# A second layer's modulation vectors, moved from the context's stages to the first layer's latent attention, in half-width blocks

## The chip, the cores and the metric

The kernel runs on one core of a Trainium2 chip. A core has five engines that work side by side, each with an instruction queue of its own: TensorE (PE, matrix products; its weight loads are listed apart as PEld), VectorE (DVE), ScalarE (ACT), GpSimd (POOL) and SyncE (SP), which here issues nearly all loads and stores. The metric is the time of one execution in microseconds (us) on the device.

## What is computed

Two layers of a diffusion backbone over 512 latent tokens and 256 context tokens of 1024 channels. Cut to what matters:

```python
for l in range(2):
    mod_lat = silu(c) @ w_ada[l] + b_ada[l]            # six vectors of 1024 for the latent tokens
    mod_ctx = silu(c_ctx) @ w_ada[l] + b_ada[l]        # and six for the context
    sh1, sc1, g1, sh2, sc2, g2 = split(mod_lat)
    xn = rms(x, norm1_g[l]) * (1 + sc1) + sh1          # modulated norm; the same for the context
    y_lat, y_ctx = token_mix(xn, hn, ...)              # attention, pooling, recurrence (mLSTM)
    x = x + g1 * (y_lat @ w_out[l])
    x = x + g2 * peer(rms(x, norm2_g[l]) * (1 + sc2) + sh2, ...)   # 16384 experts, product-key routing
    # in the first layer the context goes the same way
```

The change concerns `silu(c) @ w_ada[l] + b_ada[l]` of the second layer (l = 1): a matrix of 1024 x 6144 numbers in float32 (24 MB), applied to two vectors.

## The kernel before

`main` (L1498) traces the program. Work is written as Python generators, each `yield` a step, and these are advanced beside each other; a planner then orders the instructions on every engine at build time by their priority in the program and by what it takes to be ready. So the order on an engine isn't exactly the program's.

The generator `ada` (L268) computes the modulation vectors of one layer. A part is one of the six vectors; a block is half a part, 512 columns. For each block it loads 1024 x 512 weights (`wa`, 2 MB, three buffers, two loads ahead), multiplies them with the two conditioning vectors on PE (eight blocks of rows, four of them side by side in a quarter of the array each), copies the sums to `row` on ACT or DVE, and sums the four quarters with small products on PE. Shifts and scales (parts 0, 1, 3, 4) become columns in `modT`, by an addition on DVE; gates (parts 2 and 5) become rows `gr`, with a bias row `bb` that is loaded, and are stored to DRAM (`grow`). The sums take one of four banks `mm` and one of two banks `tr` of PSUM, which all other work in this stage uses too. Every product goes through `mm` (L142), every load and store by SP through `load` (L200), every copy through `copy` (L130, L132).

In the first layer `main` does this (L1508 to L1540):

1. Context: its norm, then `ada` parts 0 and 1 of layer 0, then its projections. `self.bg` holds a chain of the rest of layer 0's `ada` (8 blocks) and all of layer 1's (12 blocks). Each step of the projections advances it by 0.7 steps, each step of the core (the context's attention `na_core` and recurrence `mlstm` in turn) by 0.5; `run(ada)` finishes it.
2. `project_ctx`: the context's output projection. From here to the end of the context's routing (`peer_ctx`) the latent generator `lat` (projections, gates, then `na_core` of the latent tokens, 20 steps) advances in the background, by the amount of foreground products.
3. A loop over what is left of `lat`, the latent attention; each step advances the recurrence `rest` of the latent tokens by 0.4 steps.
4. `project`: the output projection of the latent tokens, with the remaining recurrence inside it; then `peer_lat`, the experts, which takes most of the layer.

A step of `na_core` has three kinds of PE work: `scores` (products of `qT` with `kT` and with the context's `kTc`), `turn` (transposes of the softmax `prob` into `probT`) and `values` (products of `probT` with V). Its softmax runs on DVE, ACT and POOL. For each new head pair `head` loads two `bias` tiles.

SBUF tiles come from pools on two stacks, left and right. A pool opened later lies above, and takes over the place of pools closed before it once their last users are done. In stage 1 the pools of `ada` are on the right. The recurrence of step 3 and `px` (the latent stream `xt`) are on the left.

Of the kernel before, what the change touches and what calls it, by code (L numbers as in the profile page):

```python
# [19 lines left out]
DRAM = bass.MemoryType.DRAM  # L20

P = 128
D = 1024
# [18 lines left out]
# latent tokens whose experts are computed densely, per layer; the rest gathers expert rows  # L42
# [22 lines left out]
# candidate pairs (a, b) of two sorted lists with (a + 1)(b + 1) <= 16: (first a, number of a, number of b, offset)  # L65
# [10 lines left out]
def merge(*gens):  # L76
    """Steps of several generators in turn."""
    gens = list(gens)
    while gens:
        for g in list(gens):  # L80
            try:
                yield next(g)
            except StopIteration:
                gens.remove(g)


class Kern:
# [57 lines left out]
    def tick(self, us):  # L145
        """Advance the background work by what fits beside `us` of foreground work."""
        if self.rate and self.bg:
            self.clock += us * self.rate
            while self.clock >= 1.0 and self.bg:
                self.clock -= 1.0  # L150
                self.step()
# [18 lines left out]
    def steps(self, n):  # L170
        """Advance the background work by n steps."""
# [5 lines left out]
    def flush(self):  # L177
        """Finish the gathers under way without starting others."""
# [5 lines left out]
    def advance(self, n):  # L184
        """Advance the second background work by n steps."""
# [29 lines left out]
    # ------------------------------------------------------------------ setup  # L215
# [34 lines left out]
    def xsrc(self, l, w, seg, i, cols=slice(0, D)):  # L250
        """Residual stream before sub-layer w of layer l: 128 tokens of a segment."""
# [15 lines left out]
    # -------------------------------------------------------------------- ada  # L267
    def ada(self, l, parts, pw, ps):  # L268
        """Modulation vectors: shifts and scales as columns, gates as rows in DRAM."""
        nc, a = self.nc, self.a  # L270
        slot = {0: 0, 1: 1, 3: 2, 4: 3}

        def fetch(j):
            w = self.T(pw, [P, KD, 512], tag="wa", bufs=ADA_BUFS)
            self.load(w, a["w_ada"][l, :, j * 512:(j + 1) * 512].rearrange("(k p) n -> p k n", p=P))
            return w

        order = [2 * part + half for part in parts for half in range(2)]
        ahead = [fetch(order.pop(0)) for _ in range(ADA_BUFS - 1)]
        for part in parts:  # L280
            for half in range(2):
                j = 2 * part + half
# [3 lines left out]
                # a quarter of the array for each of four blocks of the contraction  # L286
                acc = self.ps("mm")
# [3 lines left out]
                row = self.T(ps, [P, 512], tag="row")  # L291
                self.copy(row, acc)
                pt = self.ps("tr")
                if part in slot:
                    for q in range(4):
                        self.mm(pt[:, q * 2:q * 2 + 2], row[:, q * P:(q + 1) * P], self.sel)
                    nc.vector.tensor_add(
                        self.modT[l][:, slot[part], half * 4:half * 4 + 4, :],
                        pt[:, :8].rearrange("p (k v) -> p k v", v=2),
                        self.bcols[:, l, part, half * 4:half * 4 + 4, None].to_broadcast([P, 4, 2]))  # L300
                else:
                    bb = self.T(ps, [2, 512], tag="bb")
                    self.load(bb, a["b_ada"][l:l + 1, j * 512:(j + 1) * 512].to_broadcast([2, 512]))
                    self.mm(pt[:2], self.sel, row)
                    gr = self.T(ps, [2, 512], tag="gr")
                    nc.vector.tensor_add(gr, pt[:2], bb)
                    self.load(self.grow[l][part // 5][:, half * 512:(half + 1) * 512], gr)
# [7 lines left out]
    # ------------------------------------------------------------ adaLN norms  # L315
    def parts(self, pool, src, cols, tag, eng, bufs):
        """Half a block of weights in the two parts that float32r products carry: a pair for each 128 rows."""
# [7 lines left out]
    def norm(self, l, w, seg, xT, xt=None, side=None, deep=2):  # L325
        """Modulated norm, channel-major, of the residual stream, in one part or two.

        xt: the stream [P, n / P, D] and partial sums of its squares [P, n / P, 4], where those are on chip."""
# [40 lines left out]
    # ------------------------------------------------------------- token mix  # L369
# [3 lines left out]
    def store(self, l, seg, full, st, m, alias=False):  # L373
        """What outlives the projections, in a pool for each of three stacks."""
# [25 lines left out]
    def projections(self, l, seg, full, m):  # L400
        """The projections of a segment, a generator that takes a block of weights in each step."""
# [17 lines left out]
    def latent(self, l, m):  # L419
        """The first layer's latent projections, then their attention where the projections' operand was."""  # L420
# [6 lines left out]
    def mlstm(self, l, seg, full, m):  # L427
        """The recurrence after the projections, a generator."""
# [12 lines left out]
    def project_ctx(self, l, m):  # L441
        """The context's new residual stream, to DRAM."""
# [20 lines left out]
    def project(self, l, m, px, sd, rest=()):  # L463
        """The latent tokens' new residual stream, to DRAM and to a pool, after the rest of their mixing."""
# [41 lines left out]
    def weights(self, l, full, pool):  # L506
        """Blocks of columns of w_in (256, the gates 100), each a step; half a block ahead of its use."""
# [20 lines left out]
    def mm3(self, out, lhs, rhs):  # L528
        """Contraction over blocks of operands that are given in two parts each."""
# [1139 lines left out]
```

## Time and profile before

| | |
|---|---|
| median of 3 runs | 4576.12 us (4574.12 to 4580.28) |
| span of the profiled execution | 4588.3 us |
| PE busy | 4041.2 us (88%) |
| DVE busy | 3483.2 us (76%) |
| POOL busy | 2233.7 us (49%) |
| ACT busy | 1761.3 us (38%) |
| HBM traffic | 216 GB/s over the span |
| PE's mean granted clock | 0.932 of full speed |

The profile comes from one execution. Its page cuts the span into 40 slices of 115 us; a digit is the busy share in tenths. The granted clock of PE is a share of 2.4 GHz. A view of windows gives the busy time of each engine in a stretch; a timeline gives start, length, engine, line, operation, the tile written and the tiles read, how many instructions were merged (x), and in brackets how long the engine stood idle before and what ended that. The ends of products are modelled, so the distance of starts tells more than a length.

### The profile page before, as it was taken

To read this page: it belongs to the slowest core of one execution; us is meant where nothing else is said; L and a number is where in the kernel's file an instruction comes from. 1 tells how busy PE (TensorE), PEld (TensorE's weight loads), DVE (VectorE), ACT (ScalarE), POOL (GpSimd) and SP (SyncE) were. 2 spreads that over 40 slices of the span, in tenths; PEclk is the share of its full clock that TensorE was granted. 3 is DMA by queue.
4 is the path that set the end of the run, shared out by engine and by line. 5 is a ranking of instruction groups with operands and counts; after the bars stand their busy time and mean duration, and the time that the engine had idled before them with its cause. 6 is when DMAs were issued, how large, how long until landed. Compare 5 with 4: busy or idle time off the path is not lost. (4 is left out here: it accounts for less than half of the span.)

```text
span 4588.3 us, 57862 instructions
## 1 busy us (share of the span) xinstructions
PE 4041.2 (88%) x20829; PEld 3367.6 (73%) x20829; DVE 3483.2 (76%) x6158; ACT 1761.3 (38%) x2754; POOL 2233.7 (49%) x1552
## 2 busy tenths in 40 slices
PE   6889777877779999999999979888868899999998
PEld 4568667756657777777777768677657788888887
DVE  2545675789979999889999855674889678887776
ACT  2332243335543333333333333343246344444343
POOL 2133355776645555455555333345866344444441
PEclk8889888988889999999999989988978999999999
DMA  7663212327778888788888633223256777777784
GB/s 270 215 211 93 81 48 82 94 94 227 219 268 303 323 316 317 301 316 316 322 316 317 257 113 109 63 73 98 71 171 206 263 294 291 286 301 296 277 304 166
DMA packets 429352, 996.51 MB, mean 217 GB/s; under 512 B 31448, under 2 KB 264280, under 8 KB 375816
## 3 DMA queue, kind: packets, MB, share of 16 engines
q1 hardware_dynamic: 372760, 586.46, 37.0%
q0 software_dynamic: 56304, 406.35, 24.2%
q8 instruction: 164, 2.69, 0.2%
q14 instruction: 124, 1.02, 0.1%
HBM read 909.97 MB, written 81.17 MB: 216 GB/s over the span
## 5 line engine op out<-in xcount | busy, mean ns | idle before, releaser
L1227 POOL TENSOR_TENSOR eacc<-eacc,uv 128x1024 f32<-128x1024 f32 x189 | 587.2, 3107 | 1074.1 <-ACT uv L1226 1013.4
L1240 DVE SCALAR_TENSOR_TENSOR uv<-uv,xn 128x1024 f32<-128x1024 f32 x384 | 849.8, 2247 | 0.0
L142 PE MATMUL o<-dvh,dch 128*128 128x512 f32 x1792 | 709.0, 396 | 72.3 <-DVE do L1436 53.2
L142 PE MATMUL o<-dvh,dcl 128*128 128x512 f32 x1792 | 706.0, 394 | 0.7 <-DVE dcl L1473 0.7
L142 PE MATMUL o<-dvl,dch 128*128 128x512 f32 x1792 | 704.9, 393 | 0.0
L1258 POOL DMA_INDIRECT uv<-in_peer_uv_dram,ridx x384 | 579.7, 1510 | 137.2 <-issue 75.0
L1394 PE MATMUL h<-xh,duh 128*128 128x512 f32 (+1 forms) x1632 | 607.7, 372 | 37.2 <-ACT duh L1388 35.8
L1394 PE MATMUL h<-xh,dul 128*128 128x512 f32 (+1 forms) x1632 | 607.6, 372 | 0.4 <-DVE dul L1389 0.3
L1394 PE MATMUL h<-xl,duh 128*128 128x512 f32 (+1 forms) x1632 | 606.0, 371 | 0.0
L142 PEld LDWEIGHTS o<-dvh,dch 128*128 128x128 f32 x1792 | 337.2, 188 | 162.1 <-DVE do L1436 64.6
L142 PEld LDWEIGHTS o<-dvh,dcl 128*128 128x128 f32 x1792 | 338.2, 189 | 86.9 <-DVE dcl L1473 14.6
L142 PEld LDWEIGHTS o<-dvl,dch 128*128 128x128 f32 x1792 | 337.5, 188 | 66.7 <-DVE dvl L1462 0.3
L1394 PEld LDWEIGHTS h<-xh,duh 128*128 128x128 f32 x1632 | 312.6, 192 | 80.4 <-ACT duh L1388 36.4
L1462 DVE TENSOR_TENSOR dvl<-dv,dvh 128x1024 fp32r<-128x1024 f32 x256 | 309.8, 1216 | 62.5 <-ACT dvh L1461 62.4
L1389 DVE TENSOR_TENSOR dul<-du,duh 128x1024 fp32r<-128x1024 f32 x204 | 249.5, 1224 | 135.0 <-ACT duh L1388 128.2
L1388 ACT CAST duh<-du 128x1024 fp32r<-128x1024 f32 x256 | 267.6, 1046 | 202.7 <-PE h L1394 102.1
L1394 PEld LDWEIGHTS h<-xl,duh 128*128 128x128 f32 x1632 | 312.1, 191 | 43.6
L1394 PEld LDWEIGHTS h<-xh,dul 128*128 128x128 f32 x1632 | 311.2, 191 | 39.7 <-DVE dul L1389 1.6
L142 PE MATMUL mm<-go,gob 128*128 128x128 f16 x1792 | 239.9, 297 | 96.9 <-DVE go L1366 85.4
L1244 ACT ACTIVATE egf<-dots 128x2 f32<-128x2 f32 x192 | 39.1, 204 | 734.8 <-DVE uv L1240 734.8
L1472 ACT CAST dch<-dcf 128x512 fp32r<-128x512 f32 (+1 forms) x256 | 145.2, 567 | 437.1 <-DVE dcf L1469 434.8
L1461 ACT CAST dvh<-dv 128x1024 fp32r<-128x1024 f32 x256 | 263.2, 1048 | 112.1 <-DMA dv<-in_peer_v_dram 63.4
(356 smaller groups left out, 8785.2 us busy)
## 6 DMA issues: line engine op xcount, KB each, us to landing
du<-in_peer_ut_dram SPq DMA_DIRECT2D x256, 512.0 KB
dv<-in_peer_v_dram SPq DMA_DIRECT2D x256, 512.0 KB
Gd<-gst SPq DMA_DIRECT2D x28, 2048.0 KB
wa<-in_w_ada_dram SPq DMA_DIRECT2D x24, 2048.0 KB
w<-in_w_in_dram SPq DMA_DIRECT2D x78, 512.0 KB
dG<-Gd SPq DMA_DIRECT2D x32, 1024.0 KB
w<-in_peer_wq_dram SPq DMA_DIRECT2D x48, 512.0 KB
dG<-Gd SPq DMA_DIRECT2D x32, 768.0 KB
```

The costliest lines, as they stand in the source:

```text
L142: self.nc.tensor.matmul(out, lhsT=lhsT, rhs=rhs, start=start, stop=stop)
L1227: nc.gpsimd.tensor_add(acc[1], acc[1], V)
L1240: nc.vector.scalar_tensor_tensor(t[:, :D], t[:, :D], 1.0, xn, op0=OP.mult, op1=OP.mult, accum_out=dots[:, k:k + 1])
L1244: nc.scalar.activation(ge, x, AF.Gelu_apprx_tanh)
L1258: nc.gpsimd.indirect_dma_start(t, None, a["peer_uv"], bass.IndirectOffsetOnAxis(ap=idx[:, k:k + 1], axis=0))
L1388: nc.scalar.copy(uh, u)
L1389: eng.tensor_sub(ul, u, uh.bitcast(F32))
L1394: nc.tensor.matmul(hp[:, :nd], lhsT=lt[:, k], rhs=rt[:, k, :nd], start=n == 0, stop=n == 3 * KD - 1)
L1461: nc.scalar.copy(vh, v)
L1462: nc.vector.tensor_sub(vl, v, vh.bitcast(F32))
L1472: m1 = nc.scalar.copy(ch, cf)
```

## The change

`ada` gets the number of buffers and the width of a block as arguments (`bufs=ADA_BUFS, n=512`), and loops over columns in steps of `n`. In the context's stage only layer 0's eight remaining blocks are left in the background; the calls that advance them stay. Layer 1's six parts are computed in the loop over the latent attention, in 24 blocks of 256 columns (1 MB each) with two buffers (one load ahead), one block with each step of `lat`, and what is left right after the loop. Its two pools are opened on the left, after a first step of `rest` that opens the recurrence's pools below them. Comments are dropped from the file as well, which shifts lines.

```diff
-    def ada(self, l, parts, pw, ps):
+    def ada(self, l, parts, pw, ps, bufs=ADA_BUFS, n=512):
...
-        def fetch(j):
-            w = self.T(pw, [P, KD, 512], tag="wa", bufs=ADA_BUFS)
-            self.load(w, a["w_ada"][l, :, j * 512:(j + 1) * 512].rearrange("(k p) n -> p k n", p=P))
+        nq = n // P
+
+        def fetch(c):
+            w = self.T(pw, [P, KD, n], tag="wa", bufs=bufs)
+            self.load(w, a["w_ada"][l, :, c:c + n].rearrange("(k p) n -> p k n", p=P))
             return w
...
-        ahead = [fetch(order.pop(0)) for _ in range(ADA_BUFS - 1)]
+        order = [part * D + c for part in parts for c in range(0, D, n)]
+        ahead = [fetch(order.pop(0)) for _ in range(bufs - 1)]
         for part in parts:
-            for half in range(2):
-                j = 2 * part + half
+            for c in range(0, D, n):
                 w = ahead.pop(0)
                 if order:
                     ahead.append(fetch(order.pop(0)))
...
-                acc = self.ps("mm")
+                acc = self.ps("mm")[:, :n]
                 for k in range(KD):
                     g = 32 * (k % 4)
                     self.mm(acc[g:g + 32], self.sc[:, k, :], w[:, k, :], k < 4, k >= 4)
-                row = self.T(ps, [P, 512], tag="row")
+                row = self.T(ps, [P, n], tag="row")
                 self.copy(row, acc)
                 pt = self.ps("tr")
                 if part in slot:
-                    for q in range(4):
+                    for q in range(nq):
                         self.mm(pt[:, q * 2:q * 2 + 2], row[:, q * P:(q + 1) * P], self.sel)
...
                 else:
...
-                    self.mm(pt[:2], self.sel, row)
-                    gr = self.T(ps, [2, 512], tag="gr")
-                    nc.vector.tensor_add(gr, pt[:2], bb)
-                    self.load(self.grow[l][part // 5][:, half * 512:(half + 1) * 512], gr)
+                    self.mm(pt[:2, :n], self.sel, row)
+                    gr = self.T(ps, [2, n], tag="gr")
+                    nc.vector.tensor_add(gr, pt[:2, :n], bb)
+                    self.load(self.grow[l][part // 5][:, c:c + n], gr)
                 yield
...
-                    ada = chain(self.ada(0, (2, 3, 4, 5), pw, ps), self.ada(1, range(6), pw, ps))
+                    ada = self.ada(0, (2, 3, 4, 5), pw, ps)
                     self.bg = [ada]
...
                 rest = self.mlstm(l, 0, True, ml)
-                for _ in lat:
-                    self.some(rest, ML_CORE)
+                next(rest)
+                with ExitStack() as s2:
+                    pw, ps = self.pool(s2, "adaw", 1, side="left"), self.pool(s2, "adas", 1, side="left")
+                    ada = self.ada(1, range(6), pw, ps, 2, 256)
+                    for _ in lat:
+                        next(ada, 0)
+                        self.some(rest, ML_CORE)
+                    run(ada)
                 sl.pop().close()
```

## Rows read from the trace of the kernel before

**Rows 1.** The page: span, and busy tenths and granted clock in 40 slices

```profile
span 4588.3 us, 57862 instructions
PE   6889777877779999999999979888868899999998
PEclk8889888988889999999999989988978999999999
```

**Rows 2.** Windows: stretch, its length, busy us (x instructions) by engine, clock, DMA share, GB/s

```profile
173.00:272.00 99.00, 85.57 (x567) 51.45 (x565) 50.36 (x169) 34.53 (x86) 20.02 (x34) 0.88 0.72 245
...
200.00:264.00 64.00, 62.96 (x458) 37.81 (x462) 37.93 (x136) 24.25 (x69) 16.64 (x26) 0.97 0.77 271
```

**Rows 3.** The same windows, of instructions on tile wa, then on tile row alone

```profile
173.00:272.00 99.00, 27.73 (x192) 5.62 (x192) 0.88 0.72 245
...
173.00:272.00 99.00, 12.86 (x72) 9.15 (x72) 2.77 (x4) 4.69 (x8) 0.88 0.72 245
```

**Rows 4.** Timeline of PE in the context's core: start, us, engine, line, operation, out<-in

```profile
188.88 3.64 PE L142 MATMUL mm<-wa,sc 128*32 128x512 f32 x16
...
199.89 2.07 PE L142 MATMUL mm<-kTc,qT 128*128 128x256 f32 x4 [0.56 <-ACT qT L988]
...
215.38 1.92 PE L142 MATMUL mm<-wa,sc 128*32 128x512 f32 x16
217.23 0.49 PE L142 MATMUL sm<-va,kw 128*128 128x130 f32 x2
...
218.42 0.95 PE L142 MATMUL tr<-sel,row 128*128 128x2 f32 x8
219.30 0.66 PE L142 MATMUL sm<-probT,Vc 128*64 128x128 f32 x8
...
250.48 1.03 PE L142 MATMUL mm<-kTc,qT 128*128 128x256 f32 x4
...
254.46 1.16 PE L142 MATMUL sm<-va,ww 128*128 128x130 f32 x8
...
257.99 1.92 PE L142 MATMUL mm<-wa,sc 128*32 128x512 f32 x16
...
272.71 13.62 PE L142 MATMUL mm<-w,yT 128*128 128x256 f32 x48 [2.17 <-DMA w<-in_w_out_dram]
```

**Rows 5.** Windows of the latent attention, columns as in rows 2

```profile
626.00:640.00 14.00, 12.83 (x101) 9.72 (x100) 10.41 (x27) 8.52 (x23) 6.76 (x11) 0.96 0.74 187
640.00:690.00 50.00, 49.11 (x408) 41.06 (x407) 40.68 (x109) 27.09 (x66) 24.42 (x25) 1.00 0.12 32
690.00:740.00 50.00, 37.63 (x259) 35.54 (x260) 37.00 (x105) 13.17 (x24) 27.59 (x24) 0.86 0.25 80
600.00:626.00 26.00, 12.87 (x69) 8.77 (x68) 24.27 (x60) 6.67 (x17) 19.27 (x24) 0.69 0.23 61
```

**Rows 6.** Timelines of DVE and of SP's queue at the end of the context's core

```profile
263.04 1.13 DVE L860 SCALAR_TENSOR_TENSOR yT<-tr,mng,og 128x128 f32<-128x128 f32 x4 [0.17 <-PE tr L197]
...
264.65 0.88 SPq L200 DMA_DIRECT2D w<-in_w_out_dram  x1
267.76 3.77 SPq L200 DMA_DIRECT2D grow<-gr  x2
```

**Rows 7.** Timelines of PE and of SP's queue in the latent attention

```profile
636.53 0.66 PE L142 MATMUL sm<-probT,VW 128*64 128x128 f32 x8
637.02 0.61 PE L142 MATMUL sm<-probT,Vc 128*64 128x128 f32 x8
...
700.18 2.10 PE L142 MATMUL sm<-va,ww 128*128 128x130 f32 x8 [4.58 <-DVE dn L819]
...
622.84 2.51 SPq L200 DMA_DIRECT2D xt<-in_x_dram  x4
...
686.23 43.52 SPq L200 DMA_DIRECT2D w<-in_w_out_dram  x7
```

**Rows 8.** Timeline of POOL at the start

```profile
0.99 0.55 POOL L638 MEMSET gif<- 36x256 f32 x2
```

More of the change, by code (lines that the diff above doesn't have):

```diff
@@ L1 @@
 from contextlib import ExitStack
-from itertools import chain
 import numpy as np
@@ L265, in xdst @@
                        ap=[[D, 16], [GW * D, GR], [1, cols.stop - cols.start]])
-    def ada(self, l, parts, pw, ps):
+    def ada(self, l, parts, pw, ps, bufs=ADA_BUFS, n=512):
         nc, a = self.nc, self.a
         slot = {0: 0, 1: 1, 3: 2, 4: 3}
-        def fetch(j):
-            w = self.T(pw, [P, KD, 512], tag="wa", bufs=ADA_BUFS)
-            self.load(w, a["w_ada"][l, :, j * 512:(j + 1) * 512].rearrange("(k p) n -> p k n", p=P))
-            return w
-        order = [2 * part + half for part in parts for half in range(2)]
-        ahead = [fetch(order.pop(0)) for _ in range(ADA_BUFS - 1)]
+        nq = n // P
+        def fetch(c):
+            w = self.T(pw, [P, KD, n], tag="wa", bufs=bufs)
+            self.load(w, a["w_ada"][l, :, c:c + n].rearrange("(k p) n -> p k n", p=P))
+            return w
+        order = [part * D + c for part in parts for c in range(0, D, n)]
+        ahead = [fetch(order.pop(0)) for _ in range(bufs - 1)]
         for part in parts:
-            for half in range(2):
-                j = 2 * part + half
+            for c in range(0, D, n):
                 w = ahead.pop(0)
@@ L294, in ada @@
                 if part in slot:
-                    for q in range(4):
+                    for q in range(nq):
                         self.mm(pt[:, q * 2:q * 2 + 2], row[:, q * P:(q + 1) * P], self.sel)
+                    ks = slice(c // P, c // P + nq)
                     nc.vector.tensor_add(
-                        self.modT[l][:, slot[part], half * 4:half * 4 + 4, :],
-                        pt[:, :8].rearrange("p (k v) -> p k v", v=2),
-                        self.bcols[:, l, part, half * 4:half * 4 + 4, None].to_broadcast([P, 4, 2]))
-                else:
-                    bb = self.T(ps, [2, 512], tag="bb")
-                    self.load(bb, a["b_ada"][l:l + 1, j * 512:(j + 1) * 512].to_broadcast([2, 512]))
-                    self.mm(pt[:2], self.sel, row)
-                    gr = self.T(ps, [2, 512], tag="gr")
-                    nc.vector.tensor_add(gr, pt[:2], bb)
-                    self.load(self.grow[l][part // 5][:, half * 512:(half + 1) * 512], gr)
+                        self.modT[l][:, slot[part], ks, :],
+                        pt[:, :2 * nq].rearrange("p (k v) -> p k v", v=2),
+                        self.bcols[:, l, part, ks, None].to_broadcast([P, nq, 2]))
+                else:
+                    bb = self.T(ps, [2, n], tag="bb")
+                    self.load(bb, a["b_ada"][l:l + 1, part * D + c:part * D + c + n].to_broadcast([2, n]))
+                    self.mm(pt[:2, :n], self.sel, row)
+                    gr = self.T(ps, [2, n], tag="gr")
+                    nc.vector.tensor_add(gr, pt[:2, :n], bb)
+                    self.load(self.grow[l][part // 5][:, c:c + n], gr)
                 yield
```

## Prediction, made before the changed kernel was run

> **What bounds the kernel now.** I read the page first: the span and the slices of the TensorE (PE) and of its granted clock [rows 1]. PE is busy 88% of the span, and the first seven slices (115 us each) hold everything the change touches: the context's first sub-layer, the latent tokens' projections beside the context's routing, then the latent attention. Nothing after about 770 us is edited. So two stretches have to be priced, and the question for each is whether PE is the limit there.
>
> The first is the context's core (attention and recurrence of the context), about 200 to 264 us. The view of windows gives PE 62.96 us of 64, VectorE (DVE) 37.93, and 271 GB/s of loads [rows 2]: PE sets the pace. The 12 blocks of the second layer's modulation vectors start at 188.88 us, and the last of them ends just ahead of 272.71 [rows 4]; in 173 to 272 their products take 27.73 us of PE and the small products on `row` behind them 12.86 us, of 85.57 us busy in all [rows 2, 3]. The timeline of PE shows how they lie in the queue: a full block at 215.38 lets the next product start 1.85 us later, its transposes at 218.42 hold the queue for 0.88 us [rows 4], together 2.73 us, and the engine goes from one to the next without a gap.
>
> The second is the latent attention, where the blocks go. From 640 to 690 us PE is busy 49.11 us of 50 at clock 1.00, with DVE at 40.68; from 626 to 640 PE has 12.83 of 14 [rows 5]. So the blocks go from one stage that PE limits to another one. Idle PE lies at its two ends: 13.1 us in 600 to 626, where DVE is busy 24.27 of 26 us with the end of the context's routing, and 12.4 us in 690 to 740, where the recurrence's last steps hang on DVE [rows 5].
>
> **What is removed from the context's core.** Of the 12 blocks, nine lie between 200 and 263 us: 9 x 2.73 = 24.6 us of a queue that is full. Without them 62.96 - 24.6 = 38.4 us of PE remain, and about 33 of DVE (37.93, less 2.77 for copies of `row` [rows 3] and about as much for the additions behind them, an estimate). PE is therefore still the largest, but no longer without gaps: the attention's softmax and the recurrence's chain become visible. I go by the distance of the attention's steps: eight steps of scores start from 199.89 to 250.48 us [rows 4], 7.2 us each. One block less in each gives 7.2 - 2.73 = 4.5; in 626 to 640, a mixed stretch without any of these blocks, PE is 92% busy [rows 5], and 4.5 / 0.92 = 4.9. Eight steps (seven distances and the outputs behind the last) save 8 x 2.3 = 18 us. Bounds: nothing hidden, 24.6; a step of 6 us, 9.6. I take 18, since PE has 38 us of work against 33 of DVE and the queue has nothing else to wait for in order.
>
> The core's tail saves nothing: from the last products at 254.46 to the last of `yT` at 263.04 [rows 4, 6] a chain of short DVE operations runs, and the block at 257.99 lay beside it. The last two blocks and their gates come after it and beside the wait for the output projection's weights: those are issued at 264.65 and PE starts on them at 272.71 [rows 4, 6], 8.1 us for 1 MB. At 271 GB/s [rows 2] 1 MB takes 3.9 us; the rest is the second layer's blocks still in flight. Saved: 4 us (0 to 5). SP's queue also stood 3.77 us at the two stores of `gr` at 267.76 [rows 6], with the context's rows, the latent tokens' x and the next weights queued behind; without them the latent norm comes forward. Saved: 3 us (0 to 6). The first block at 188.88 takes 3.64 us at half clock beside the gates' chain on DVE: nothing (0 to 2). Together **-25 us**, with ends at -10 and -37. What is late next is the context's output projection, which simply starts earlier, and all behind it shifts with it.
>
> **What is added to the latent attention.** Each block becomes two of 256 columns. A half block keeps 16 product instructions (8 row blocks, two passes each) of half the columns, and has half of the transposes. Half of 2.73 is 1.37 us. The instruction count could set a floor: eight products on `probT` let the next eight start 0.49 us later (636.53 to 637.02 [rows 7]), 0.061 us each, so 16 take 0.98 us, and with 0.5 for the transposes 1.5 us. I take **1.4 us**, near the first end, as 0.93 us of columns for 16 instructions is just under that floor. 24 of them are 33.6 us (33 to 36).
>
> How many fall in the loop follows from the code. The ticks in `project_ctx` (64 products of 0.427 us at rate 0.2: 5.5) and in the routing (16 x 3.84 us at 0.25: 15.4) advance the latent generator 20 steps. It has 17 before the attention and 20 in it, so 17 steps remain in the loop, and 17 half blocks go with them; 7 are left for `run(ada)` behind the loop.
>
> Loop: 17 x 1.4 = 23.8 us, less the idle PE of 626 to 690, 1.2 + 0.9 us [rows 5]: **+22 us**. The 13.1 us idle in 600 to 626 I don't count as cover: the pool of the weights stands on the left stack above `px` and the recurrence's tiles, and `px`'s loads are issued from 622.84 us on [rows 7], when the routing's tiles there are done. The first half block would so arrive at about 628. If its place were free earlier, up to 9 half blocks could fit, -13.
>
> Behind the loop: 7 x 1.4 = 9.8 us in 12.4 us of idle PE. Half of it finds the gaps where the recurrence waits for DVE (one is 4.58 us, at 700.18 [rows 7]), some pushes that chain: **+3 us** (0 to 9.8).
>
> The rest: 24 copies of `row` on ACT and DVE, additions, and on SP 24 loads of 1 MB, 8 of `bb`, 8 stores of `gr`. DVE has 9 us spare in 640 to 690, DMA is 12% busy there [rows 5]. Waits are the danger: with two buffers a load waits on SP until the block before the last has been multiplied, and behind it are queued `bias` for the next head and, after 686.23, the output projection's weights [rows 7]. The store of `gr` waits for DVE in the same queue. PE then waits for `bias` through POOL and DVE. I take **+2 us** (0 to 8). Together **+27 us**, with ends at +12 and +44.
>
> Nothing else changes: the eight blocks of the first layer stay in the context's projections, and the second layer's vectors are needed only in the second layer, far behind.
>
> **Sum.** -25 + 27 = +2 us. The profiled execution took 4588.3 us [rows 1], 0.27% above the median of 4576.12 (4574.12 to 4580.28); the sum is a difference of stages and goes on the median: **4578 us**. A measurement of this kernel tells about 0.2% (9 us) from no change.
>
> **Rivals.** *The gaps take more than I count* (faster). The order on an engine is not the program's but a planner's, which pulls ready work forward: POOL clears the recurrence's `gif` at 0.99 us [rows 8], some 100 us before its use. If it puts four or five half blocks into 600 to 626 (-7), all seven last ones into 690 to 740 (-3), and the latent norm into the now open ends of the context's core (-6), the change is worth -14: 4562. For it: 25 us of idle PE at the right places. Against: the left stack's place seems not free before 622 us.
>
> *The clock falls in the context's core* (slower). Where PE is busy half of the time, its granted clock is lower: 12.87 of 26 us at 0.69 in 600 to 626, against 1.00 in 640 to 690 [rows 5]. The core would keep 38.4 us of work in some 46, 83%, and decides by whether its gaps are bunched. Should it get 0.75, the 38.4 us become 51: even a full queue would save only 13 us, with the chains' waits 10 (a step of 6 us), and the latent norm could no longer use the 3 us: -10 - 4 + 0 + 27 = +13, 4589. The point from which it decides is a clock below about 0.85 between 200 and 250 us. The Trainium skill, "TensorE: Matmul & The Clock Gate" (Part 1: The HAM clock gate), says that the throttled clock is the default and only sustained work lifts it, so that work taken out of a stream can make what is left slower. By that rule these blocks were also what kept the core at 0.97, and the time would be the 4589 of this rival. The rows bear it out in part: the stretch 626 to 640, 92% busy, still has 0.96.
>
> *The two buffers hold up SP's queue* (slower). If a load regularly stands in front of `bias` or the output projection's weights, three heads lose 3 us each and the weights 4: +2 + 13 = 4591. It decides when half blocks come faster than 1 MB lands (3.9 us at 271 GB/s, 8.1 at worst [rows 2, 4, 6]); steps of about 5.9 us speak against it.
>
> *It doesn't do what it says*: the planner lets most half blocks drift behind the loop. Then 33.6 us less the 12.4 idle, +21 in place of +27: 4572, no change either.
>
> **How the numbers follow.** Forecast 0.40, drift 0.04: within 0.2% together 0.44. Gaps 0.28: faster. Clock 0.20 and queue 0.08: slower 0.28. The range takes in the two outer cases with some of their spread: 4556 to 4597; the likeliest case alone spans 4568 to 4587.
>
> **What would show it.** In the profile after: no 512-wide products on `wa` behind about 173 us; score steps of the context about 4.9 us apart at a clock above 0.9; the context's output projection starting near 250 and not at 272.71; 384 products of 256 columns on `wa` between about 628 and 730; the attention's PE-full stretch some 22 us longer. Wrong: context steps of 6 us or a clock below 0.85 (rival two), half blocks before 620 (rival one), SP's `bias` landing late with PE waiting on DVE's addition (rival three). The forecast falls if either stretch is off by more than 9 us without the other following.

## The result and the profile after

The changed kernel takes 4614.89 us (median of 4 runs, 4611.04 to 4617.29), against 4576.99 us of the kernel before beside it: a ratio of 1.008 with a 95% interval from 1.0066 to 1.0095. It is 38 us slower, and lies above the forecast's range.

The page after shows little of it: against [rows 1], TensorE's busy tenths fall in the fifth slice (461 to 577 us) and rise in the sixth and the eleventh; the differences in the 25th to 27th come from all work there being later.

```profile
span 4614.4 us, 58329 instructions
...
PE   6889687877879999999999978978868899999998
...
PEclk8889888888889999999999989989878999999999
```

To find the 38 us I follow four marks through both traces: the end of the context's routing on TensorE (the last transposes of its `xT`), the last scores of the latent attention (`kT`,`qT`), the issue of `gB` (output projection of the latent tokens) and the issue of `iotac` (start of the latent tokens' routing). The first and last mark before:

```profile
598.41 0.62 PE L197 MATMUL tr<-ident,xT 128*128 128x128 f32 x4
...
773.40 0.33 SPq L200 DMA_DIRECT2D iotac<-in_iota_dram  x1
```

The two between, before, on TensorE's timeline and on SyncE's queue (the second of the pair of score products starts at 675.8):

```profile
675.56 0.59 PE L142 MATMUL mm<-kT,qT 128*128 128x256 f32 x2
...
685.86 0.33 SPq L200 DMA_DIRECT2D gB<-grow  x1
```

All four, after (start, length, engine, line, operation, tile written and read, instructions merged; brackets: idle time before, and what ended it), on TensorE's timeline:

```profile
193.04 3.16 PE L141 MATMUL mm<-kTc,qT 128*128 128x256 f32 x8
...
224.99 1.03 PE L141 MATMUL mm<-kTc,qT 128*128 128x256 f32 x4
...
246.66 22.20 PE L141 MATMUL mm<-w,yT 128*128 128x256 f32 x94 [0.50 <-DMA w<-in_w_out_dram]
...
566.16 0.63 PE L196 MATMUL tr<-ident,xT 128*128 128x128 f32 x4
566.62 0.43 PE L196 MATMUL tr<-ident,kk 128*128 128x128 f32 x2
...
567.76 0.38 PE L196 MATMUL tr<-ident,kk 128*128 128x128 f32 x2
...
589.32 1.11 PE L196 MATMUL tr<-ident,kk 128*128 128x128 f32 x4 [19.72 <-ACT kt L131]
...
598.31 1.94 PE L141 MATMUL mm<-wa,sc 128*32 128x256 f32 x16 [3.21 <-issue]
...
606.59 1.07 PE L141 MATMUL mm<-wa,sc 128*32 128x256 f32 x16
607.59 0.70 PE L141 MATMUL mm<-kT,qT 128*128 128x256 f32 x2
...
608.55 0.50 PE L141 MATMUL tr<-sel,row 128*128 128x2 f32 x4
608.92 0.68 PE L141 MATMUL mm<-kT,qT 128*128 128x256 f32 x2
...
673.59 0.59 PE L141 MATMUL mm<-kT,qT 128*128 128x256 f32 x2
...
706.05 1.07 PE L141 MATMUL mm<-wa,sc 128*32 128x256 f32 x16 [0.86 <-DMA wa<-in_w_ada_dram]
707.74 1.02 PE L141 MATMUL tr<-sel,row 128*128 128x2 f32 x4 [0.61 <-DVE row L129]
709.26 1.94 PE L141 MATMUL mm<-wa,sc 128*32 128x256 f32 x16 [0.50 <-DMA wa<-in_w_ada_dram]
```

and on SyncE's queue:

```profile
239.35 0.43 SPq L199 DMA_DIRECT2D w<-in_w_out_dram  x1
...
589.84 1.01 SPq L199 DMA_DIRECT2D wa<-in_w_ada_dram  x2
...
677.72 33.90 SPq L199 DMA_DIRECT2D wa<-in_w_ada_dram  x9
...
726.00 0.35 SPq L199 DMA_DIRECT2D gB<-grow  x1
...
805.19 0.33 SPq L199 DMA_DIRECT2D iotac<-in_iota_dram  x1
```

Read in order:

- **The context gave 32 us.** Its output projection starts at 246.66 and not at 272.71 [rows 4], and its routing ends at 566.16 and not at 598.41: 26 us at the projection and 6 more by the routing's end.
- **The attention took 30 us back.** The last scores stood at 675.8 us before and stand at 673.8 now (the second of the pair at 673.59). Two things are new. TensorE stands still for 19.72 us, for a copy of the recurrence's transposed keys. And twelve half blocks lie in it, the first at 598.31; the scores of the loop's first step ran at 565, ahead of that stop.
- **The stretch behind the attention took 42 us.** `gB` was issued at 685.86 before, 10 us behind the last scores; now at 726.00, 52 us behind, and the output projection's weights of [rows 7] at 726.41. Twelve half blocks lie in it, and ten loads of `wa` are issued in it.
- **8 us came back** from `gB` to `iotac`: 87.5 us before, 79.2 now. Part of the recurrence had run among the blocks: TensorE has 65 us of work in 726 to 805, against 73 in 686 to 773.4 before.

That is -32 + 30 + 42 - 8 = +32 us up to 805.19. What follows hasn't changed; its length in the profiles of all variants below (but the two that move the blocks into it) is 3801 to 3815 us, the kernel before at the upper end with 3814.9. So the rest of the 38 us is the spread of single executions: the profiled one of the kernel before was itself above its median.

The windows after (stretch, length, busy us with instructions for PE, PEld, DVE, ACT, POOL, then clock, DMA share, GB/s) answer to [rows 2, 5]:

```profile
220.00:246.00 26.00, 18.19 (x111) 13.13 (x110) 18.21 (x67) 10.96 (x32) 12.57 (x18) 0.75 0.24 69
600.00:640.00 40.00, 39.48 (x336) 29.88 (x332) 24.43 (x69) 18.19 (x44) 14.66 (x16) 0.94 0.81 248
640.00:674.00 34.00, 34.00 (x299) 24.13 (x299) 23.63 (x66) 15.82 (x38) 12.80 (x14) 1.00 0.57 191
674.00:726.00 52.00, 44.53 (x396) 29.09 (x395) 18.22 (x61) 9.37 (x22) 5.84 (x8) 0.87 0.62 203
700.00:720.00 20.00, 14.01 (x130) 6.21 (x126) 4.31 (x16) 1.49 (x4) 1.08 (x1) 0.81 0.81 264
```

and the products on `wa` alone (PE, PEld, clock, DMA share, GB/s):

```profile
568.00:674.00 106.00, 13.71 (x192) 5.28 (x192) 0.87 0.59 187
674.00:726.00 52.00, 16.52 (x192) 5.96 (x192) 0.87 0.62 203
```

192 instructions are 12 half blocks: twelve lie ahead of the last scores and twelve behind them. That is the program's order. The loop has 17 steps left, but only the first 13 of them compute scores (two more have transposes and values, the last two nothing), and block k is traced behind step k. So the 13th to the 17th block stand behind the last scores together with the seven of `run(ada)`. In 703 to 720 nothing but these blocks runs on TensorE, and in 700 to 720 the DMA engines are busy 81% of the time.

### The profile page after: what moved, and what is told of

Its sections match the earlier page's. It is cut to its first block, busy times and chain, and to the rows that moved or that the text cites. A ratio compares the mean times of both kernels' runs of the same rounds, so it can differ in the third digit from the quotient of the medians.

```text
span 4614.4 us, 58329 instructions
## 1 busy us (share of the span) xinstructions
PE 4053.0 (88%) x21029; PEld 3381.1 (73%) x21029; DVE 3485.8 (76%) x6174; ACT 1763.0 (38%) x2762; POOL 2236.2 (48%) x1552
```

## Experiments

Each kernel was run beside the kernel before (median 4576 to 4580 us), and a loss or gain is the difference to that median; a ratio's interval is some 0.0010 to 0.0017 to either side, 5 to 8 us.

**What leaving the context is worth, and what the early first step costs.** The second layer's blocks are left out (the second layer takes the first one's vectors, so the output is another), without and with `next(rest)` ahead of the loop:

```diff
-                next(rest)
-                with ExitStack() as s2:
...
-                    for _ in lat:
-                        next(ada, 0)
-                        self.some(rest, ML_CORE)
-                    run(ada)
+                self.modT[1], self.A[1], self.grow[1] = self.modT[0], self.A[0], self.grow[0]
+                for _ in lat:
+                    self.some(rest, ML_CORE)
```

> The kernel before without the second layer's modulation blocks anywhere: no products, no loads, no bias or gate rows; the second layer takes the first layer's vectors instead, which costs nothing. The recurrence's first step stays where it was before. This measures what leaving the context's stages gives by itself. Theory (the context's stages gave 32 us, and everything lost lies in the attention and behind it): 4577 - 32 = 4545 us. Rival (the context's gain is partly lost again before the attention, because the routing's end on VectorE sets its start): 4577 - 20 = 4557 us or more.

> As the kernel without the second layer's blocks, but with the recurrence's first step traced ahead of the loop over the latent attention, as the change does. Theory (key transposes that come early hold both small PSUM banks while their copies wait for a place in SBUF, 19.7 us in the profile after the change): 20 us above the kernel without blocks, 4565 us. Rival (TensorE would have waited there in any case, for the attention's first products or for the end of the routing): within 5 us of the kernel without blocks.

Measured: without blocks 4547.88 us (ratio 0.9931, 0.9914 to 0.9947), 32 us under the kernel before; with the early step 4559.32 us (0.9955, 0.9938 to 0.9971), 11 us more. The first is as the theory had it, the second lies halfway between theory (20) and rival (within 5). The waits of TensorE in 540 to 800 us of the second kernel (total, times, longest) have a line that the first doesn't have:

```profile
PE tr L196 <- ACT kt L131: 19.7, 1, 19.7
```

But the first kernel waits in that stretch too, 13 us in all (1.7, 5.0, 4.0 and 2.4, between 568 and 590), for the softmax and the scaled queries; two of these lines:

```profile
PE mm L141 <- ACT qT L988: 5.0, 1, 5.0
...
PE tr L196 <- POOL prob L1013: 4.0, 1, 4.0
```

So 19.7 us of standing still delay the attention by 7: from the routing's end to the last scores it takes 84.7 us and not 77.3.

How the stall comes about can be read in the trace after: the planner pulls two pairs of the key transposes (`tr<-ident,kk`) to 566.62 and 567.76. They fill both `tr` banks. The first copies out of them (`kt`) run at 588.9, just behind the routing's last operation on VectorE (`ridx`, 588.66). That its tiles lie where `kt` goes is inferred from these times, and from `stt`, a tile of the same pool, whose clearing on GpSimd was released by `ridx`:

```profile
588.89 0.37 ACT L131 COPY kt<-tr 128x256 f32<-128x256 f32 x1 [1.21 <-issue]
...
588.93 1.40 POOL L741 MEMSET stt<- 128x1560 f32 x1 [2.94 <-DVE ridx L1187]
```

The next transposes in TensorE's queue need a `tr` bank, and everything behind them waits, attention included.

**Undoing the early step, and running the last blocks beside the recurrence**, each alone:

```diff
-                next(rest)
+                next(lat)
+                next(lat)
+                self.some(rest, 2 * ML_CORE)
...
+                    next(ada)
+                    next(ada)
                     for _ in lat:
```

```diff
-                    run(ada)
+                    for _ in ada:
+                        self.some(rest, 0.6)
```

> The changed kernel with the recurrence's first step back behind two steps of the latent attention; the pools of the modulation weights open after it, two half blocks are done at that point, 15 in the loop, and 7 behind it as before. Theory (the early key transposes cost 20 us): 4615 - 20 = 4595 us, and no wait of TensorE for the copies of the transposed keys over 5 us between 560 and 600 us. Rival (TensorE then waits for something else there, such as the first weights, which can't land before the routing's tiles are free): 4610 to 4615 us.

> The changed kernel with the seven half blocks behind the loop taken in turn with the recurrence's steps (0.6 step for each block), where the change runs them one after another ahead of the recurrence. Theory (the blocks' chain of load, products, copy, transposes and gate rows stands in front of the recurrence, though both fit beside each other): of the 40 us between the last attention product and the output projection's weights 20 to 30 come back, 4585 to 4595 us. Rival (the stretch is set by the weights' loads, 4 to 5 us for 1 MB each, and by the single tile of gate bias rows, whatever is traced beside them): the same loads take the same time, 4608 to 4615 us.

Measured: 4615.68 us (1.0078, 1.0061 to 1.0095) and 4615.73 us (1.0078, 1.0061 to 1.0095). Neither gives anything, against my theory in both cases. In the first the wait for `kt` is gone, but TensorE is no busier in that place. Windows of 577 to 595, the first kernel with the undone step, then the one without blocks:

```profile
577.00:595.00 18.00, 3.91 (x11) 2.18 (x10) 17.45 (x23) 3.99 (x9) 12.23 (x7) 0.58 0.19 53
```

```profile
577.00:595.00 18.00, 10.25 (x35) 7.30 (x36) 16.54 (x30) 5.55 (x13) 10.95 (x10) 0.55 0.40 105
```

My edit had put two half blocks between two attention steps, ahead of the scores that fill this time in the kernel without blocks; the last set below takes them away from there. In the second, `gB` goes out even later (732.04 and not 726.00), and `iotac` earlier (797.11 and not 805.19): the recurrence does run among the blocks, for 8 us in the profile that the median doesn't confirm.

**Without the loads, and with one more buffer.**

```diff
         def fetch(c):
+            if n == 256 and len(kept) == 2:
+                kept.append(kept.pop(0))
+                return kept[1]
             w = self.T(pw, [P, KD, n], tag="wa", bufs=bufs)
+            kept.append(w)
             self.load(w, a["w_ada"][l, :, c:c + n].rearrange("(k p) n -> p k n", p=P))
```

```diff
-                    ada = self.ada(1, range(6), pw, ps, 2, 256)
+                    ada = self.ada(1, range(6), pw, ps, 3, 256)
```

> The changed kernel, but of the second layer's 24 half blocks only the first two are loaded; the other 22 multiply these two again, so 22 MB of loads are left out and every product, copy and transpose stays. Theory A (the loads set the pace: 24 MB can only start at 590 us, and 1 MB takes about 4 us at the 250 GB/s of 700 to 720 us): most blocks fall back into the loop and the last ones follow each other faster; with 24 blocks of 1.4 us on TensorE above the kernel that has none but keeps the early first step (4559 us), 4559 + 34 = 4593 us. Theory B (TensorE's own chain sets it: product, wait for the copy of the row, transposes, at a clock that falls in the gaps): 4610 to 4615 us, and the last blocks still about 3.5 us apart.

> The changed kernel with three buffers of weights and not two, so two loads ahead. If two buffers make each load wait for the product of the block before the last (latency, not bandwidth): the blocks behind the attention go from 3.8 us to about 3 us each and one or two more fit into the loop, 4600 to 4605 us. If bandwidth or TensorE's chain sets the pace: 4612 to 4617 us.

Measured: without 22 of the loads (so the output is wrong) 4595.67 us (1.0046, 1.003 to 1.0063), 18 us less of a loss than the change; with three buffers 4605.16 us (1.0067, 1.0051 to 1.0084), about half of that. The times are as the theory of the loads had them. Its "most blocks fall back into the loop" didn't come: without loads, too, twelve blocks lie ahead of the last scores (at 669.85 us) and the 13th behind them, at 672.86. So the loads don't decide how many blocks lie in the attention. The products on `wa`, in 13 blocks and then in 11:

```profile
590.00:674.00 84.00, 14.30 (x208) 5.50 (x208) 0.95 0.25 70
674.00:704.00 30.00, 14.15 (x176) 5.94 (x176) 1.00 0.01 2
```

The marks place the 18 us. The way from the routing's end to the last scores is as long without loads (107.2 us) as with them (107.6). The one from there to `gB` is 42 us and not 52, and the one to `iotac` 74 and not 79; the other 3 us lie ahead of the first of these loads and belong to the spread of single executions. Without loads the blocks follow each other in a full queue behind the attention, at full clock:

```profile
674.00:712.00 38.00, 36.43 (x369) 26.22 (x368) 17.04 (x60) 8.08 (x18) 5.97 (x7) 1.00 0.01 2
```

With three buffers the issues behind the attention come closer, 24.88 us for eight and not 33.90 for nine, 3.6 us from one to the next and not 4.2:

```profile
675.02 24.88 SPq L199 DMA_DIRECT2D wa<-in_w_ada_dram  x8
```

**The two edits together, with two buffers and with three, and without loads.**

> The changed kernel with both edits that gave nothing alone: the recurrence's first step behind two steps of the attention, and the blocks behind the loop in turn with the recurrence's steps. If each edit's gain was hidden by the other's loss (the early transposes' 20 us only moved the waiting to the first weights; the overlap of 8 us up to the routing was real): 4600 to 4607 us. If something third sets the stretch, such as the loads from 590 us on: 4612 to 4617 us.

> The changed kernel with three buffers, the recurrence's first step behind two steps of the attention, and the blocks behind the loop in turn with the recurrence. If the pace of the loads is what hides the gains of the other two edits: about 10 for the buffers and 5 to 10 for the others, 4595 to 4600 us, still slower than before. If three buffers take all there is: 4603 to 4607 us.

> The kernel with 22 of the 24 loads left out, and with the recurrence's first step back behind two steps of the attention. That step cost 11 us where there are no blocks and nothing where there are blocks with their loads. Theory (the loads hid it: without early transposes TensorE waited for weights that can't land sooner): without loads it is worth its 11 us again, 4596 - 11 = 4585 us. Rival (it isn't the loads but the blocks themselves that fill that time): 4593 to 4598 us.

Measured: 4609.63 us (1.0076, 1.0059 to 1.0094), 4603.58 us (1.0054, 1.004 to 1.0068) and 4594.65 us (1.0041, 1.0028 to 1.0054). The first lies between its two expectations and settles nothing. The second is just inside "three buffers take all there is": a loss of 27 us, against 29.5 with the buffers alone. The third goes to the rival: with the undone step the loss is 18 us, without it 20. So it isn't the loads that hide the step's price. What is left is how I undid it.

**The step undone without blocks ahead of the loop** (the two lines with `next(ada)` are left out, so nine half blocks stand behind the loop), with the loads, without them, and with three buffers and the last blocks beside the recurrence:

> As the changed kernel with the recurrence's first step back, but the two half blocks that stood ahead of the loop are left to its end, so nine half blocks are behind it. Theory (the early step's cost is real, and the two early blocks and their pools, put between two attention steps that had no weights yet, took its place: TensorE stood idle from 577 to 595 us behind them): without early blocks the 11 us come back, less two more blocks of 3.8 us behind the loop, 4615 - 11 + 4 = 4608 us. Rival (what the loads cost hides it in any case): 4613 to 4619 us.

> The same order with 22 of the 24 loads left out. Theory (the 11 us of the early step and the 19 us of the loads add up): 4596 - 11 = 4585 us, that is 24 blocks at 1.5 us on top of the 4548 us of the kernel without blocks. Rival (blocks in this stretch cost near 2 us each even without loads, because they take the banks and the in-order queue from the softmax and the recurrence): 4593 to 4598 us.

> The same order with all loads, with three buffers, and with the blocks behind the loop in turn with the recurrence. If the three costs are separate (11 for the early step, 10 for the buffers, up to 8 for the recurrence): 4588 to 4597 us, still slower than before by the 2 us of my sum and what is left of the loads. If they hide each other: 4600 to 4606 us.

Measured: 4610.35 us (1.0065, 1.0049 to 1.0082), 4588.87 us (1.0017, 1.0007 to 1.0027) and 4598.03 us (1.0041, 1.0029 to 1.0054), that is 32, 10 and 19 us above the kernel before; each lies between its two expectations, a little nearer to the theory. Without loads, the step's 10 us are there (20 to 10), so the two early blocks of the earlier edit had covered them (18 with them, 10 without). With the loads it is 6 us (38 to 32), which the intervals can't tell from none. All three edits bring the loss to half, 19 us. If the buffers' 8 and the step's 10 add up, as these times allow, nothing is left for the blocks in turn with the recurrence; no run has the first two edits alone, so that isn't shown. The kernel without loads also keeps the program's order: two steps of the attention are traced ahead of its loop, and ten blocks (160 instructions) lie ahead of the last scores, at 659.7:

```profile
560.00:660.00 100.00, 10.71 (x160) 4.17 (x160) 0.91 0.25 72
```

The marks of the kernel without loads and of the one with them differ by 18 us at `iotac`:

```profile
781.84 0.33 SPq L199 DMA_DIRECT2D iotac<-in_iota_dram  x1
```

```profile
800.30 0.33 SPq L199 DMA_DIRECT2D iotac<-in_iota_dram  x1
```

**Another place for the blocks**: the latent tokens' routing (800 to 1000 us before the change), where TensorE had some idle time and DMA little to do. First behind the routing (one block ahead of it, then three with each of eight steps of early experts), then one or two blocks ahead of each of its 16 projections; the pools of `ada` are opened ahead of the routing and closed before the dense gates are built.

```diff
-            self.advance(TAIL[l])
+            for i in range(TAIL[l]):
+                self.advance(1)
+                if l + 1 < DEPTH:
+                    for _ in range(3):
+                        next(ada, 0)
```

```diff
                         self.advance(ROUTE[l])
+                        for _ in range(1 + j):
+                            next(self.side, 0) if self.side else None
```

> The second layer's blocks neither in the context's stages nor at the attention: the same 24 half blocks with two buffers are traced behind the latent tokens' routing, three with each of the eight steps of early experts, before the dense gates are built; the recurrence's first step is back where it was before. There TensorE was busy 36 to 42 of each 50 us before the change, with VectorE and GpSimd as the limit. Theory (a block costs what TensorE hasn't idle): the 34 us of the blocks lie in 30 us or more of idle time, 4548 (the kernel without blocks) plus 0 to 15, 4548 to 4563 us. Rival (the blocks push the early experts into the stretch that TensorE limits, and are paid in full): 4548 + 34 = 4582 us or more.

> As the kernel with the blocks beside the routing, but traced inside it: one or two of the 24 half blocks ahead of each of the 16 projections of the latent tokens' routing, and not behind it. There the loads found 0.2 to 0.3 of the DMA engines busy and TensorE 119 of 150 us. Theory (blocks cost what TensorE hasn't idle, if loads and blocks are spread over the stretch): 4548 (the kernel without blocks) plus 5 to 20, 4553 to 4568 us, faster than before by 0.2 to 0.5%. Rival (TensorE and VectorE take turns there in one chain, so each block lengthens it): 4548 + 34 = 4582 us or more.

Measured: 4619.58 us (1.0096, 1.0078 to 1.0114) and 4598.29 us (1.0045, 1.0032 to 1.0058): losses of 44 and 22 us, 76 and 54 us more than the kernel without blocks, both to the rival's side. In the first, the blocks stand in a row behind the routing, paced by their loads (TensorE waits for them 35 us in all, 14 at most); from 1000 to 1100 us TensorE is half idle at 343 GB/s, and the dense gates wait for the end of it:

```profile
1000.00:1100.00 100.00, 51.03 (x316) 25.23 (x316) 44.61 (x79) 18.41 (x35) 38.91 (x22) 0.62 0.95 343
```

In the second they are spread, and the stage from `iotac` to the load behind the routing (`iotag`) shows that the idle time wasn't used. Without blocks, then with them:

```profile
739.50:976.70 237.20, 192.07 (x809) 151.99 (x809) 173.40 (x860) 73.98 (x149) 182.16 (x188) 0.86 0.27 83
```

```profile
739.00:1018.60 279.60, 229.40 (x1242) 167.76 (x1243) 194.76 (x889) 79.94 (x164) 179.50 (x187) 0.90 0.48 151
```

TensorE has 37 us more to do and the stage is 42 us longer: its idle time has grown from 45 to 50 us, and none of the blocks went into it. The idle time there was the routing's own chain from product to VectorE and GpSimd and back. A block brings a link of its own into it: TensorE now waits for VectorE's copies of `row`, which stand behind the routing's operations there, up to 8.3 us for one, and VectorE itself waits up to 6.4 us for a bias row `bb`. No run took this work off VectorE, so what that alone costs is open.

```profile
PE tr L142 <- DVE row L130: 10.7, 6, 8.3
```

No place that I tried beats the kernel before.

## Why the prediction was wrong

What failed is the sum for the latent attention: +27 was forecast and about +70 measured. Three of its terms were too small. The half blocks were counted as partly hidden in idle time and weren't; the loads were put at next to nothing; and the early first step of the recurrence had no term at all. The runs give a number for each (differences to the kernel before; every one has an interval of 5 to 8 us to either side, and as each term is a step from one kernel to the next, that they add up to 38 is no check):

| term | forecast | measured | from |
|---|---|---|---|
| leaving the context | -25 | -32 | kernel without blocks |
| 24 half blocks, no loads, no early step | +25 (22 and 3) | +42 | no loads and step undone (10) less no blocks (-32) |
| the early first step | not priced | +10 | no loads, with the step (20) and without (10) |
| the loads | +2 (all waits) | +18 | the change (38) less no loads (20) |

Two other kernels give the second and third term again: with the early step in both, no loads less no blocks is 20 + 21 = 41, and without blocks the step costs 11.

- **The context: right in the main term, in part by luck in the rest.** -32 lies inside the ends -10 and -37. Seven distances of score steps shrank from 50.6 us to 31.95 (193.04 to 224.99; 32 to 36 in the profiles of the variants, whose context is the same): 4.6 us a step where 4.9 was forecast, and 18.6 us where 18 was. The tail, put at 4 us, gave 0.6: 21.7 us from the last scores to the output projection, and 22.2 before. The weights took 7.3 us (239.35 to 246.66) with no block in flight, so the 8.1 us weren't the blocks' doing. The start, put at 0 to 2, gave 7: the first scores came at 193.04 and not at 199.89 (187 to 196 in the variants, which is the spread of single executions). And 6 us more came up to the routing's end, with the latent norm's transposes now ahead of the output projection, where 3 were forecast.
- **The rival *clock falls* didn't come.** In the context's attention the clock stayed at 0.97, and TensorE was still 92% busy. The 0.75 of 220 to 246 us is the tail behind it, where TensorE waits 5.6 us for the recurrence's last chain and has 8 us of work in 15:

```profile
193.00:231.00 38.00, 35.03 (x238) 26.46 (x238) 32.83 (x129) 21.72 (x65) 16.01 (x24) 0.97 0.09 25
231.00:246.00 15.00, 7.73 (x34) 5.23 (x30) 7.96 (x27) 5.78 (x15) 6.65 (x10) 0.57 0.41 119
```

  The Trainium skill, "TensorE: Matmul & The Clock Gate" (Part 1: The HAM clock gate), says that activity releases the throttle, and both rows agree with that. The core at 0.75 that the rival needed wasn't there.

- **The number of blocks in the loop: the count was right, the place it was priced for was not.** "17 half blocks go with them; 7 are left" is how the program and the trace have it. But the last four of the 17 steps compute no scores, so five of the 17 blocks fall behind the last scores, into the stretch that was to hold seven: twelve and twelve. The first weights came at 598 where the forecast had about 628; less the 32 us of the context, that is the same place. The sign "half blocks before 620" for the rival *gaps* came only by this shift, and no block lay beside the end of the routing.
- **No block was hidden.** Ahead of the last scores that was as forecast: with ten blocks there and no loads, the way from the routing's end to the last scores is 91.4 us, against 77.3 without blocks, 1.4 us for a block. Behind them it wasn't. "Half of it finds the gaps where the recurrence waits for DVE" was +3 for seven blocks; fourteen blocks and no loads made the stretch to `gB` 35 us longer, of which 11 came back up to `iotac`: 25 us, 1.8 for a block. The rival *it doesn't do what it says* had many blocks behind the loop, and took all 12.4 us of idle time off them. In the trace the last six run one after another from 702.97 us on, and the recurrence's next products stand behind them in TensorE's queue (720.68). But taking the two in turn gave nothing, so no run shows that this order is the cause.
- **The loads.** Behind the attention the blocks follow their 1 MB loads, issued 4.2 us apart, against 1.4 to 1.5 us of products and transposes. The forecast had this price (3.9 us for 1 MB) and put it into the rival *two buffers* only, as delay of others' loads, with the condition "when half blocks come faster than 1 MB lands". In the loop, with a block every 5.4 us or more, they don't, and the loads cost nothing there; behind it they do. The output projection's weights, too, were issued only at 726.41, behind all of them. That rival had the right place and nearly the right price of a load, and too small a chance; its 4591 was still 24 us short, for it had neither the step nor the cost of the blocks themselves.
- **The half block: right.** In the loop most of those for shifts and scales take 1.37 us of the queue (606.59 to 607.59 and 608.55 to 608.92), gates 1.53, some of the late ones 1.54 (676.59 to 677.59 and 678.17 to 678.71). 16 products start 0.0625 us apart, as the bound by instruction count had it. 24 of them are 33 to 37 us, and the forecast had 33 to 36.
- **The early first step: not priced at all.** The diff shows `next(rest)` ahead of the loop, and I read it as opening pools. It also makes the recurrence's first transposes older than the attention's next ones, so the planner puts them first, at a time when their copies have no place in SBUF. The prediction knew the fact that it needed: places on the left stack come free only with the routing's tiles.

What stays open: with the loads in, undoing the step brought 6 us and not 10; the intervals are too wide to say whether step and loads overlap. The two kernels that give the step's 10 us differ by two blocks in the loop besides. Why a block behind the attention costs 1.8 us without loads, where its products and transposes are 1.4 to 1.5, was not taken apart. And no run had full-width blocks in the loop, so what the half width gives or costs isn't known.

## What to carry to other kernels

Count moved work against what each step of the loop holds: the last steps of a software pipeline are half empty, and work hung on them lies behind it. Loads that need a place which is freed late don't use the idle time ahead of it, and what stands in a row behind the loop ran here at the pace of the loads, not of the products. A generator's first step that only "opens pools" also makes its instructions old; look at what they hold (here both `tr` banks) until the copy behind them has a place. Idle time of an engine inside another chain isn't free: with 37 us of added products the routing's stage grew by 42, and its 45 us of idle TensorE by 5. Compare whole stages, from mark to mark: in a fixed window of a slower kernel, less of the work lies in it.

## What I had not expected of the hardware

Behind the attention the granted clock is 0.87 with the loads (674 to 726 us) and 1.00 without them (674 to 712), for nearly the same products. With the loads TensorE's work there is broken by gaps of 0.5 to 1.4 us, at the weights and at the copies of `row`. The half block at 709.26 us takes 1.94 us at a clock of 0.50 (1.2 GHz), the one before it, at 706.05, 1.07 us at 1.00 (2.4 GHz). So a late load is paid twice, once as a wait and once as a slower product behind it: of the 10 us that this stretch is longer, about 6 are idle time and 4 are slower products, an estimate from the busy times in the two windows.
